# Writing down the order of GpSimd's work in the up-projection of a hybrid diffusion backbone

## The chip, the cores and the metric

The kernel runs on one core of a Trainium2 chip. The metric is device time in microseconds (us) of one execution. The engines are named as in the profile: PE (matrix products), DVE (VectorE), ACT (ScalarE), POOL (GpSimd) and SP, whose queue issues most DMAs. Each engine takes its own instructions in the order in which they stand in its stream, and waits at an instruction until the semaphores of that instruction are there.

## The reference, cut to what matters

One layer of a trunk over 2048 latent tokens of width 1024, with 256 tokens of context in front. All inputs are float32. The change lies in the last third of the layer, the gated MLP with a depthwise 3x3 convolution on the activation branch:

```python
def conv_ffn(h, w_up, taps, conv_b, w_down, rows):
    a, g = jnp.split(h @ w_up, 2, axis=-1)          # (2048, 1024) @ (1024, 2 * 2816)
    bsz, t, f = g.shape
    g2, tp = g.reshape(bsz, rows, GRID_W, f), taps  # rows of 64 tokens
    gc = lax.conv_general_dilated(g2, tp[:, :, None, :].astype(g.dtype), (1, 1), 'SAME',
                                  dimension_numbers=('NHWC', 'HWIO', 'NHWC'), feature_group_count=f)
    gc = gc.reshape(bsz, t, f) + conv_b
    return (a * jax.nn.gelu(gc, approximate=False)) @ w_down
```

## The kernel before

**Stages.** Input projection and the two token mixers (tiles `pj`, `sc`, `mi`), then the output projection with the second norm, then the up-projection `h @ w_up` (tiles `up`, `Ah`, `Al`), then the down-projection (tile `dn`, `mhl`, `thl`). Every product of two float32 matrices is made of three passes of a rounded type: each operand is split into a high part (a cast on ACT) and a low part (raw minus high), and high x high, high x low and low x high are summed in PSUM.

**The up-projection.** The tokens are done in two halves of 1024 (`hh` 0 and 1). Each half goes through 22 units, 11 of the gate `g` and 11 of the value `a`, each for 256 columns of `w_up`. A unit is a fast matrix product with seven products (`i` 0 to 6) in place of eight: column quarters of the weights, `a11`, `a12`, `a21`, `a22`, and sums of them are multiplied with stored combinations of the activations (`xah`, `xal`, `yfar`), 12 matmuls of 128x512 for each product. There are 308 products. A gate unit and a value unit run interleaved, 14 products for the two; such a stretch is called a **round** below. A round of 14 products makes the gate of two blocks of 128 channels and the value of the two blocks whose gate came out of the round two before.

**Preparing the weights** (`Unit.prep`, called three products ahead: `LOOK = 3`, four buffers each of `Ah` and `Al`). For product `i` of a unit ACT casts the operand to `Ah` (L125) and POOL subtracts it to get `Al` (L126). Besides, POOL makes the sums of quarters, in place: L1251 after `i` = 0, L1253 (`s2`, seen as tile `s` for a gate unit and `fl` for a value unit) after 1, L1255 (a11 = s2 + a11) after 2, L1257 (a12 = a12 - s2) after 3. The operand of `i` = 2 is `s2`; that of `i` = 3 is the a11 that L1255 leaves; that of `i` = 5 is the a12 that L1257 leaves.

**After a product** (`after`). DVE and ACT add the PSUM bank (four banks `up`) into the rows `gp` for the convolution (L1524) or into the value. Of a value unit, products `i` = 1 and 4 are multiplied with the gate on DVE (L1531, L1532); for `i` = 5 and 6 DVE adds (L1534) and POOL multiplies into the gate's tile `cv` (L1535), and the block is stored to `m`.

**The convolution** (`conv`). For each block of 128 channels ACT starts it with the first tap (L1433, into the PSUM tile `dn`, two buffers), DVE does the other eight taps (L1436), ACT applies the GELU (L1452 in the first half, L1457 in the second) into one of three tiles `cv`. In the second half DVE also makes three small edge taps (L1440) for each block. Each round has two of these convolutions.

**What sets the order.** The kernel's text emits all this in one sequence, but a scheduler places each engine's instructions by its own estimate, except those that are wrapped in `pin(...)` (`tc.keep_in_program_order`): these keep the order in which they are written among the pinned ones of their engine. Before the change on POOL in this stage L1253, the memset L1455 and the product of edges L1458 are pinned.

Of the kernel before, what the change touches and what calls it, by code (L numbers as in the profile page):

```python
# [9 lines left out]
F32 = mybir.dt.float32  # L10
# [67 lines left out]
def tile_trunk(ctx, tc, x, c, cx, c_ctx, w_ada, b_ada, norm_mix, norm_ffn, w_in, hg_norm, sgu_g, sgu_b,  # L78
               w_sp, b_sp, w_out, w_up, conv_w, conv_b, w_down, norm_final, masks, out):
    nc = tc.nc  # L80
    V, S, G, T = nc.vector, nc.scalar, nc.gpsimd, Tensor(nc.tensor)
    ld = nc.sync.dma_start
    st = nc.sync.dma_start
    pin = tc.keep_in_program_order
# [38 lines left out]
    def split(hi, lo, raw, eng=None, keep=lambda i: i):  # L123

        keep(S.copy(hi, raw))  # L125
        (eng or G).tensor_sub(lo, raw, hi.bitcast(F32))  # L126
# [57 lines left out]
    with es1:  # L184
# [169 lines left out]
        with tc.manual_schedule():  # L354
# [30 lines left out]
            for k in range(NK):  # L385
                for i in range(2):
                    o = (k % 2) * 256 + i * P
# [249 lines left out]
        def need(q, what):  # L637
            while what not in done:
                if hg_q.soon:
                    hg_q.flush()  # L640
                    continue
                assert q.tasks
                q.step()
# [531 lines left out]
        i = len(seq) - 4  # L1175
# [34 lines left out]
    def a_tiles():  # L1210
        return tuple(px.tile([P, 4, P], F32R, tag=w, name=w, bufs=4, align_bytes=AL) for w in ("Ah", "Al"))
# [4 lines left out]
    def c_tile():  # L1216
        return px.tile([P, NK, P], F32R, tag="fl", name="fl", bufs=2, align_bytes=AL)
# [5 lines left out]
    class Unit:  # L1223
# [15 lines left out]
        def prep(self, i):  # L1239

            a11, a21 = self.raw[0][:, :, :P], self.raw[0][:, :, P:]
            a12, a22 = (self.raw[1][:, :, :P], self.raw[1][:, :, P:]) if i else (None, None)
            self.A[i] = a_tiles()
            hi, lo = self.A[i]

            if i == 1:
                self.s2 = (c_tile()[:, :4, :].bitcast(F32) if self.slots[0] == 1 else
                           px.tile([P, 4, P], F32, tag="s1", name="s2"))
            split(hi, lo, (a11, a12, self.s2, a11, a21, a12, a22)[i])
            if i == 0:  # L1250
                G.tensor_sub(a21, a11, a21)  # L1251
            elif i == 1:
                pin(G.tensor_sub(self.s2, a22, a21))  # L1253
            elif i == 2:
                G.tensor_add(a11, self.s2, a11)  # L1255
            elif i == 3:
                G.tensor_sub(a12, a12, self.s2)  # L1257

    units = []
    for hh in range(2):  # L1260
# [25 lines left out]
    with tc.tile_pool(name="po", bufs=1, reuse_waits="tile") as po:  # L1286
# [62 lines left out]
        for t, (hh, g) in enumerate(tiles):  # L1349
# [15 lines left out]
            o = ops.pop(t)  # L1365
# [5 lines left out]
            if t + 1 == nt_:  # L1371
                for n in range(3):
                    prep(n)
# [36 lines left out]
    def g_rows(hh, f, n2):  # L1410

        return view(gp[f % 4], (1 + 2 * n2) * RW + 1, [[4 * RW, 4], [RW, 2], [1, GW]])

    def v_cols(hh, f, n2):
        return view(vals[hh, f], hh * GW + n2 * P, [[2 * P, 4], [1, P]])
# [4 lines left out]
    def edge(hh, f):  # L1420

        e = edges[:, f % 4]
        if hh:
            ld(e[:, 0, :], gs_d[f][:, 1, :])
            ld(e[:, 1, :], as_d[f])
        return e

    def conv(hh, f, e):

        gt = gp[f % 4]  # L1430
        cp = dbank().rearrange("p a b -> p (a b)")
        cr = cp.rearrange("p (r c) -> p r c", c=GW)
        S.activation(cr, gt[:, 0:RH, 0:GW], AF.Identity, bias=cvb[:, f:f + 1], scale=taps[:, f:f + 1])  # L1433
        yield
        for t in range(1, 9):
            V.scalar_tensor_tensor(out=cr, in0=gt[:, t // 3:t // 3 + RH, t % 3:t % 3 + GW],  # L1436
                                   scalar=taps[:, t * NF + f:t * NF + f + 1], in1=cr, op0=ALU.mult, op1=ALU.add)
            if hh and t == 4:
                for tt in range(6, 9):
                    V.scalar_tensor_tensor(out=e[:, 0, :], in0=gt[:, 1, tt % 3:tt % 3 + GW],  # L1440
                                           scalar=taps[:, tt * NF + f:tt * NF + f + 1], in1=e[:, 0, :],
                                           op0=ALU.mult, op1=ALU.add)
            if hh and t == 6:
                pin(S.activation(e[:, 0, :], e[:, 0, :], AF.Gelu))
            yield
        tapped.add((hh, f))
        while out_v[0] == 3:
            yield "full"
        out_v[0] += 1
        vt = v_tile()  # L1450
        if hh == 0:
            pin(S.activation(vt[:, :TH - GW], cp[:, :TH - GW], AF.Gelu))  # L1452
            S.copy(e[:, 0, :], cp[:, TH - GW:])
            S.dma_start(gs_d[f][:, 1, :], e[:, 0, :])
            pin(G.memset(vt[:, TH - GW:TH], 1.0))  # L1455
        else:
            pin(S.activation(vt[:, GW:], cp, AF.Gelu))  # L1457
            pin(G.tensor_mul(vt[:, :GW], e[:, 0, :], e[:, 1, :]))  # L1458
        vals[hh, f] = vt
        yield  # L1460
# [27 lines left out]
    def put_m(hh, f):  # L1488
        stores.append((now[0] + 3, hh, f))
# [13 lines left out]
    def quad(p, kind):  # L1503
        return p.rearrange("p (j c) -> p j c", c=P) if kind == "a" else p.rearrange("p (j r c) -> p j r c", r=2, c=GW)

    def after(u, i, p):

        hh, f, kind = u.hh, u.f, u.kind
        if i == 0:
            t = pf.tile([P, 2 * 512], F32, tag="keep", name="keep", bufs=2)  # L1510
            u.u, u.u3 = t[:, :512], t[:, 512:]
            S.copy(u.u, p)
            return
        if i == 2:
            V.tensor_add(u.u, p, u.u)
            return
        if i == 3:
            V.tensor_add(u.u3, p, u.u)
            return
        c, n2, add = {1: (0, 0, u.u), 4: (1, 1, u.u3), 5: (0, 1, u.u3), 6: (1, 0, u.u)}[i]  # L1520
        if kind == "g":
            if f >= 4:
                need(tapped, (hh, f + c - 4))
            V.tensor_add(g_rows(hh, f + c, n2), quad(p, kind), quad(add, kind))  # L1524
        else:
            need(vals, (hh, f + c))
            o = v_cols(hh, f + c, n2)
            if i < 5:
                if i == 4:
                    V.tensor_add(u.u, p, u.u)  # L1530
                V.tensor_add(p, p, add)  # L1531
                V.tensor_mul(o, quad(p, kind), o)  # L1532
            else:
                V.tensor_add(add, p, add)  # L1534
                G.tensor_mul(o, quad(add, kind), o)  # L1535
                put_m(hh, f + c)
        if kind == "g" and i == 4:
            V.tensor_add(u.u, p, u.u)
        if kind == "g" and i == 6:
            for ff in (f, f + 1):  # L1540
                if hh == 0:
                    st(gs_d[ff][:, 0, :], gp[ff % 4][:, RH, 1:GW + 1])
                else:
                    ld(gp[ff % 4][:, 0, 1:GW + 1], gs_d[ff][:, 0, :])
                fresh.append(conv(hh, ff, edge(hh, ff)))
# [41 lines left out]
    for n, (u, i) in enumerate(prods):  # L1587
# [5 lines left out]
        hi, lo = u.A[i]  # L1593
# [5 lines left out]
        if n == 12:  # L1599
            edges = px.tile([P, 7, P], F32R, tag="yst", name="edges", bufs=2, align_bytes=AL).bitcast(F32)  # L1600
            edges = edges[:, :4, :].rearrange("p f (w c) -> p f w c", w=2)
        after(u, i, p)
        put_stores(n)
        for j in range(7):
            if last_use[j] == n - 4:
                for w in range(2):
                    load_b(1, j, w)
        prep(n + LOOK)
        if n == NP - 8:
            ts = [c_tile().rearrange("p a b -> p (a b)").bitcast(F32) for i in range(2)]  # L1610
# [263 lines left out]
```

## Time and profile before

| what | us |
|---|---|
| median of 3 runs (2397.96 to 2403.45) | 2401.12 |
| the profiled execution: its own time | 2401.11 |
| its span, first to last instruction | 2399.3 |
| what lies around the span | 1.8 |
| first and last matmul of the up-projection, from the span's start | 1121.56, 1971.52 |
| granted clock of PE, mean | 0.994 |

All lines in the prediction are from this one profiled execution. A line of the timeline reads: start, length, engine, line of the kernel, operation, output and inputs, shape, and in brackets how long the engine stood idle just before and what it waited for. Two pieces of the same kind are often one line with a count (x2). A length contains a short tail that overlaps the next instruction, so the time that an instruction takes of its engine is better read from one start to the next.

### The profile page before, as it was taken

To read this page: it belongs to the slowest core of one execution; us is meant where nothing else is said; L and a number is where in the kernel's file an instruction comes from. 1 tells how busy PE (TensorE), PEld (TensorE's weight loads), DVE (VectorE), ACT (ScalarE), POOL (GpSimd) and SP (SyncE) were. 2 spreads that over 40 slices of the span, in tenths; PEclk is the share of its full clock that TensorE was granted. 3 is DMA by queue.
4 is the path that set the end of the run, shared out by engine and by line. 5 is a ranking of instruction groups with operands and counts; after the bars stand their busy time and mean duration, and the time that the engine had idled before them with its cause. 6 is when DMAs were issued, how large, how long until landed. Compare 5 with 4: busy or idle time off the path is not lost.

```text
span 2399.3 us, 38726 instructions
## 1 busy us (share of the span) xinstructions
PE 2347.8 (98%) x14951; PEld 1936.3 (81%) x14951; DVE 1705.8 (71%) x2331; ACT 977.3 (41%) x1762; POOL 798.4 (33%) x739
## 2 busy tenths in 40 slices
PE   6999999999999999999999999999999999999998
PEld 5887887878887887887788888887888888888887
DVE  4655667556668652666898787689999984776876
ACT  4674443443445452544433333333333333232343
POOL 0020000010211021004687877878787860000011
PEclk9999999999999999999999999999999999999999
DMA  8364443584435536678522222642222259844744
GB/s 307 120 199 151 141 124 126 167 279 153 159 128 178 188 110 222 202 242 289 185 85 92 82 92 93 242 172 85 87 95 87 86 175 343 269 145 134 251 154 168
DMA packets 305428, 396.39 MB, mean 165 GB/s; under 512 B 33609, under 2 KB 216657, under 8 KB 302557
## 3 DMA queue, kind: packets, MB, share of 16 engines
q1 hardware_dynamic: 301956, 393.17, 49.4%
q8 instruction: 118, 1.93, 0.3%
q10 hardware_dynamic: 3289, 0.76, 0.1%
q14 instruction: 65, 0.53, 0.1%
HBM read 284.73 MB, written 109.13 MB: 164 GB/s over the span
## 4 chain that ended last, share of the span: by engine, by line
PE 47%; DVE 4%; POOL 1%; issue 1%; DMA 0%; ACT 0%; POOLq 0%; SPq 0%; ACTq 0%
PE up L70 30%; PE dn L70 17%; DVE dn L1436 2%; POOL Al L126 0%; DVE edges L1440 0%; DVE gp L1524 0%; DMA m<-cv 0%; POOL cv L1535 0%; DMA sT<-wd 0%; POOL raw L1257 0%; DVE cv L1532 0%; DMA yd<-fl 0%; POOL fl L1253 0%; ACT cv L1457 0%; DVE up L1531 0%
## 5 line engine op out<-in xcount | busy, mean ns | idle before, releaser
L1436 DVE SCALAR_TENSOR_TENSOR dn<-gp,taps,dn 128x1024 f32<-128x1024 f32 x352 | 449.0, 1282 | 12.8 <-ACT dn L1433 9.6
L70 PE MATMUL up<-yfar,Ah 128*128 128x512 f32 x1232 | 394.3, 390 | 2.0 <-DVE cv L1532 2.0
L70 PE MATMUL dn<-thl,mhl 128*128 128x512 f32 x1680 | 381.0, 389 | 0.0
L70 PEld LDWEIGHTS dn<-thl,mhl 128*128 128x128 f32 x1680 | 315.4, 188 | 65.5 <-issue 0.2
L70 PE MATMUL pj<-xh,whi 128*128 128x512 f32 x896 | 367.7, 411 | 0.0
L126 POOL TENSOR_TENSOR Al<-raw,Ah 128x512 fp32r<-128x512 f32 x264 | 342.4, 1308 | 68.2 <-ACT Ah L125 67.9
L70 PE MATMUL pj<-xh,wlo 128*128 128x512 f32 x896 | 351.9, 393 | 2.1 <-DVE wlo L225 2.1
L70 PE MATMUL pj<-xl,whi 128*128 128x512 f32 x896 | 351.0, 392 | 0.0
L125 ACT CAST Ah<-raw 128x512 fp32r<-128x512 f32 x264 | 162.9, 620 | 334.9 <-PE up L70 261.3
L70 PE MATMUL up<-xah,Al 128*128 128x512 f32 x704 | 275.3, 391 | 3.6 <-POOL Al L126 3.6
L70 PE MATMUL up<-xah,Ah 128*128 128x512 f32 x704 | 275.2, 391 | 0.0
L70 PEld LDWEIGHTS up<-yfar,Ah 128*128 128x128 f32 x1232 | 231.5, 188 | 50.2 <-issue 2.4
L70 PE MATMUL up<-xal,Ah 128*128 128x512 f32 x528 | 205.8, 390 | 0.0
L70 PE MATMUL up<-yfar,Al 128*128 128x512 f32 x528 | 205.5, 390 | 0.0
L70 PEld LDWEIGHTS pj<-xh,wlo 128*128 128x128 f32 x896 | 168.6, 188 | 40.2 <-DVE wlo L225 3.6
L70 PEld LDWEIGHTS pj<-xh,whi 128*128 128x128 f32 x896 | 168.8, 188 | 35.1 <-issue 3.5
L70 PEld LDWEIGHTS pj<-xl,whi 128*128 128x128 f32 x896 | 169.1, 189 | 29.0
L70 PE MATMUL dn<-wo,o 128*128 128x512 f32 x768 | 182.7, 394 | 0.8 <-DVE nt L724 0.8
L70 PEld LDWEIGHTS dn<-wo,o 128*128 128x128 f32 x768 | 142.1, 188 | 30.0 <-DVE nt L724 1.0
L70 PEld LDWEIGHTS up<-xah,Al 128*128 128x128 f32 x704 | 132.6, 188 | 32.8 <-POOL Al L126 5.2
L70 PEld LDWEIGHTS up<-xah,Ah 128*128 128x128 f32 x704 | 132.6, 188 | 27.1
L222 ACT CAST whi<-raw 128x1024 fp32r<-128x1024 f32 x68 | 71.4, 1049 | 118.7 <-PE pj L70 96.7
(322 smaller groups left out, 3635.0 us busy)
## 6 DMA issues: line engine op xcount, KB each, us to landing
raw<-in_w_up_dram SPq DMA_DIRECT2D x88, 512.0 KB, 3.7
mr<-m SPq DMA_DIRECT2D x85, 512.0 KB, 5.3
raw<-in_w_in_dram SPq DMA_DIRECT2D x68, 512.0 KB, 4.0
sT<-wd SPq DMA_DIRECT2D x88, 256.0 KB, 4.4
raw<-in_w_ada_dram SPq DMA_DIRECT2D x32, 512.0 KB, 3.7
yfar<-yd SPq DMA_DIRECT2D x14, 1024.0 KB, 19.1
m<-cv SPq DMA_DIRECT2D x22, 544.0 KB, 2.7
raw<-in_w_down_dram SPq DMA_DIRECT2D x22, 512.0 KB, 4.2
```

Source lines behind the costliest of these rows:

```text
L70: return self.engine.matmul(out, lhsT, rhs, **kw)
L125: keep(S.copy(hi, raw))
L126: (eng or G).tensor_sub(lo, raw, hi.bitcast(F32))
L222: S.copy(hi, raw)
L1436: V.scalar_tensor_tensor(out=cr, in0=gt[:, t // 3:t // 3 + RH, t % 3:t % 3 + GW], scalar=taps[:, t * NF + f:t * NF + f + 1], in1=cr, op0=A ...
```

## The change

On POOL the low parts of the up-projection's weights, the three sums of quarters that were free, and the product of gate and value are now pinned, so that they follow the order in which the kernel writes them. No instruction is added or removed, and no operand changes. `split` is written out for this, since its subtraction had no pin.

```diff
-            split(hi, lo, (a11, a12, self.s2, a11, a21, a12, a22)[i])
+            S.copy(hi, (a11, a12, self.s2, a11, a21, a12, a22)[i])
+            pin(G.tensor_sub(lo, (a11, a12, self.s2, a11, a21, a12, a22)[i], hi.bitcast(F32)))
             if i == 0:
-                G.tensor_sub(a21, a11, a21)
+                pin(G.tensor_sub(a21, a11, a21))
             elif i == 1:
                 pin(G.tensor_sub(self.s2, a22, a21))
             elif i == 2:
-                G.tensor_add(a11, self.s2, a11)
+                pin(G.tensor_add(a11, self.s2, a11))
             elif i == 3:
-                G.tensor_sub(a12, a12, self.s2)
+                pin(G.tensor_sub(a12, a12, self.s2))
...
                 V.tensor_add(add, p, add)
-                G.tensor_mul(o, quad(add, kind), o)
+                pin(G.tensor_mul(o, quad(add, kind), o))
                 put_m(hh, f + c)
```

Lines behind L1249 have a number one higher in the changed kernel (L1251 becomes L1252, L1535 becomes L1536); the cast and the subtraction, L125 and L126 before, are L1249 and L1250 there.

The first place is POOL in the second half of the up-projection, around the two products of gate and value at the end of a round (`cv<-keep,cv`). `Al_17006` is the low part for `i` = 2 of the next gate unit, `raw_16844` the first quarters of the value unit that is being prepared, `fl_17032` its `s2`. Before:

```order
L126 TENSOR_TENSOR Al_16984<-raw_16844,Ah_16983 128x512
L1535 TENSOR_TENSOR cv_16526<-keep_16732,cv_16526 128x4x128
L126 TENSOR_TENSOR Al_17006<-s2_16961,Ah_17005 128x512
L126 TENSOR_TENSOR Al_17031<-raw_16942,Ah_17030 128x512
L1253 TENSOR_TENSOR fl_17032<-raw_16942,raw_16844 128x512
L1255 TENSOR_TENSOR raw_16844<-fl_17032,raw_16844 128x4x128
L1257 TENSOR_TENSOR raw_16942<-raw_16942,fl_17032 128x4x128
L1535 TENSOR_TENSOR cv_16800<-keep_16732,cv_16800 128x4x128
```

And in the changed kernel, the same place:

```order
L1536 TENSOR_TENSOR cv_16526<-keep_16732,cv_16526 128x4x128
L1250 TENSOR_TENSOR Al_16960<-raw_16868,Ah_16959 128x512
L1254 TENSOR_TENSOR s2_16961<-raw_16868,raw_16779 128x512
L1250 TENSOR_TENSOR Al_16984<-raw_16844,Ah_16983 128x512
L1252 TENSOR_TENSOR raw_16844<-raw_16844 128x4x128
L1536 TENSOR_TENSOR cv_16800<-keep_16732,cv_16800 128x4x128
L1250 TENSOR_TENSOR Al_17006<-s2_16961,Ah_17005 128x512
L1256 TENSOR_TENSOR raw_16779<-s2_16961,raw_16779 128x4x128
L1250 TENSOR_TENSOR Al_17031<-raw_16942,Ah_17030 128x512
L1254 TENSOR_TENSOR fl_17032<-raw_16942,raw_16844 128x512
L1250 TENSOR_TENSOR Al_17055<-raw_16779,Ah_17054 128x512
L1258 TENSOR_TENSOR raw_16868<-raw_16868,s2_16961 128x4x128
```

Behind these rows stand `Al_17076` (from `fl_17032`) and then the sum L1256 on `raw_16844`. So the first product (`cv_16526`) moved ahead of two low parts that it stood behind, the second (`cv_16800`) ahead of `Al_17006` and `Al_17031`, which stood in front of it, and the value unit's sum on `raw_16844`, two instructions ahead of the second product before, now stands eight instructions behind it and thirteen behind the first. The first half has the same rows in the same order.

The second place is ACT just behind, in the changed kernel; `Ah_17115` is the cast of `raw_16844` as L1256 leaves it, and `dn_17123` the next convolution:

```order
L1249 CAST Ah_17095<-raw_16779 128x512
L1249 CAST Ah_17115<-raw_16844 128x512
L1458 ACTIVATE cv_17120<-dn_16803 128x1024
L1434 ACTIVATE dn_17123<-gp1_11526,vec_67,taps_68 128x1024
L1249 CAST Ah_17139<-raw_16868 128x512
```

Nothing moved here: in the kernel before the five rows stand in the same order. On ACT in all, the cast of `s2` and a neighbour change places four times. DVE's order is the same from its first instruction to its last, and PE's differs in the place of one matmul.

The third place is POOL near the start of the up-projection, in the second round. Before:

```order
L126 TENSOR_TENSOR Al_11930<-raw_11815,Ah_11929 128x512
L1253 TENSOR_TENSOR fl_11931<-raw_11815,raw_11721 128x512
L1255 TENSOR_TENSOR raw_11721<-fl_11931,raw_11721 128x4x128
L1257 TENSOR_TENSOR raw_11815<-raw_11815,fl_11931 128x4x128
L126 TENSOR_TENSOR Al_11954<-raw_11685,Ah_11953 128x512
```

And in the changed kernel:

```order
L1250 TENSOR_TENSOR Al_11930<-raw_11815,Ah_11929 128x512
L1254 TENSOR_TENSOR fl_11931<-raw_11815,raw_11721 128x512
L1250 TENSOR_TENSOR Al_11954<-raw_11685,Ah_11953 128x512
L1258 TENSOR_TENSOR raw_11795<-raw_11795,s2_11855 128x4x128
L1250 TENSOR_TENSOR Al_11975<-fl_11931,Ah_11974 128x512
```

The low part `Al_11954` stood behind all three sums of the value unit, and now stands behind the first of them.

## The prediction

> **What bounds the kernel now.** I read the page first, its shares and its 40 slices:
>
> ```profile
> PE 2347.8 (98%) x14951; PEld 1936.3 (81%) x14951; DVE 1705.8 (71%) x2331; ACT 977.3 (41%) x1762; POOL 798.4 (33%) x739
> ...
> DVE  4655667556668652666898787689999984776876
> ...
> POOL 0020000010211021004687877878787860000011
> ```
>
> PE is the bound of the whole span. POOL's 33% is an average that hides the stage: in slices 20 to 33 (60 us each), which are the up-projection, POOL is 60 to 80% busy and DVE up to 90% and more. The change touches only that stage. Two stretches of one round's length, one in each half:
>
> ```profile
> 1332.00:1370.00 38.00, 38.00 (x169) 31.50 (x168) 29.89 (x32) 13.95 (x22) 30.49 (x27) 1.00 0.27 86
> ...
> 1794.00:1832.00 38.00, 38.00 (x169) 31.48 (x168) 34.90 (x39) 14.20 (x22) 30.82 (x27) 1.00 0.28 90
> ```
>
> After the length come the busy times of PE, PEld, DVE, ACT and POOL. PE has no gap; POOL has 7.5 us of 38 to spare, DVE 8.1 and then 3.1. So there is next to nothing to win in the middle of the stage. What PE loses to POOL is in the groups and in PE's own waits:
>
> ```profile
> L70 PE MATMUL up<-yfar,Ah 128*128 128x512 f32 x1232 | 394.3, 390 | 2.0 <-DVE cv L1532 2.0
> ...
> L70 PE MATMUL up<-xah,Al 128*128 128x512 f32 x704 | 275.3, 391 | 3.6 <-POOL Al L126 3.6
> ...
> 1179.90 0.50 PE L70 MATMUL up<-xah,Al 128*128 128x512 f32 x1 [1.77 <-POOL Al L126]
> ...
> 1564.50 0.50 PE L70 MATMUL up<-xah,Al 128*128 128x512 f32 x1 [1.62 <-POOL Al L126]
> ```
>
> POOL is waited for 3.6 us in all, DVE 2.0. That 5.6 us, 0.23%, is the most that a better order can win here.
>
> **The change part by part.** No instruction comes or goes, so busy times stay; every term is a wait. I name the steps of a round: E1 and E2 are DVE's adds L1534 after the value unit's products `i` = 5 and 6; M1 and M2 POOL's products L1535 that need them; R the value unit's sum L1255, whose result ACT casts; C the convolution's start L1433, which stands behind that cast on ACT; S the first tap L1436 on DVE, which needs C.
>
> *Removed.* The waits at 1179.90 and 1564.50 come from a low part that stands behind three sums in a row; in the new order the sums stand between the low parts, so both fall away: -3.4 us.
>
> *Added: a loop.* The order rows show that M1, which must wait for E1, now stands thirteen instructions ahead of R, and M2 eight ahead. Before, R stood ahead of M2 and only four behind M1. R releases the cast, the cast stands ahead of C, C releases S, and DVE works in order from S to the next round's E1 and E2. That is a closed ring through DVE, POOL and ACT, once a round. It costs nothing while it is shorter than PE's round. First half:
>
> ```profile
> 1298.98 2.61 DVE L1436 SCALAR_TENSOR_TENSOR dn<-gp,taps,dn 128x1024 f32<-128x1024 f32 x2
> ...
> 1309.26 0.69 DVE L1524 TENSOR_TENSOR gp<-up,keep 128x512 f32<-128x512 f32 x1 [0.38 <-PE up L70]
> ...
> 1317.22 0.39 PE L70 MATMUL up<-xah,Ah 128*128 128x512 f32 x1
> ...
> 1317.42 0.69 DVE L1534 TENSOR_TENSOR keep<-up,keep 128x512 f32<-128x512 f32 x1
> ...
> 1321.61 1.31 POOL L1535 TENSOR_TENSOR cv<-keep,cv 128x512 f32<-128x512 f32 x1
> 1322.87 1.31 POOL L126 TENSOR_TENSOR Al<-s,Ah 128x512 fp32r<-128x512 f32 x1
> ...
> 1333.56 0.62 ACT L125 CAST Ah<-raw 128x512 fp32r<-128x512 f32 x1 [1.86 <-PE up L70]
> ...
> 1335.56 1.21 ACT L1433 ACTIVATE dn<-gp,vec,taps 128x1024 f32<-128x1024 f32 x1 [0.41 <-ACT edges L1453]
> ...
> 1337.06 2.61 DVE L1436 SCALAR_TENSOR_TENSOR dn<-gp,taps,dn 128x1024 f32<-128x1024 f32 x2
> ...
> 1714.12 0.68 DVE L1534 TENSOR_TENSOR keep<-up,keep 128x512 f32<-128x512 f32 x1
> ...
> 1714.88 1.30 POOL L1535 TENSOR_TENSOR cv<-keep,cv 128x512 f32<-128x512 f32 x1 [0.57 <-DVE keep L1534]
> ```
>
> PE's round is the time between the two first taps, 1298.98 and 1337.06: 38.08 us, or 2.72 for a product. DVE from S (1298.98) to the end of E1 (1318.11) takes 19.13, less 0.38 and 0.20 in which it waited for PE (the product ended at 1317.22): 18.55. POOL from M1 to the end of R is 14 instructions of 1.26 (the starts 1321.61 and 1322.87): 17.6. ACT from the cast to the end of C (1336.77): 3.21. Handing over costs 0.08 to POOL (1714.80 to 1714.88), and 0.03 to DVE (1835.84 to 1835.87 in the rows further down), which I take for ACT too. Sum 39.5: **longer than PE's round by 1.4 us**. PE itself feels it when M1's delay uses up the slack of the low part seven instructions on (`i` = 2 of the gate unit): it is done 0.69 + 0.08 + 7 x 1.26 = 9.6 us after E1's start. It is due for the third matmul, 0.45 us into the product that starts 4 x 2.72 after 1317.22; E1 started 0.20 after that, so it is due after 10.88 + 0.45 - 0.20 = 11.1 us: slack 1.5.
>
> ```profile
> 1242.97 0.69 DVE L1534 TENSOR_TENSOR keep<-up,keep 128x512 f32<-128x512 f32 x1
> ...
> 1507.82 0.69 DVE L1534 TENSOR_TENSOR keep<-up,keep 128x512 f32<-128x512 f32 x1
> ```
>
> These are E1 of the second and of the ninth round that have one: seven rings, 264.9 us now and 7 x 39.5 = 276.5 in the changed kernel, +11.6; less the slack of 1.5, and less 2 us because the second round's E1 comes earlier without the wait at 1179.90 (its 1.77 and a little idle time): **+8 us**, with that wait's end in it.
>
> In the second half M2 closes the longer ring, since three edge taps lie between E1 and E2:
>
> ```profile
> 1797.79 1.29 DVE L1436 SCALAR_TENSOR_TENSOR dn<-gp,taps,dn 128x1024 f32<-128x1024 f32 x1 [1.16 <-ACT dn L1433]
> ...
> 1808.74 0.69 DVE L1524 TENSOR_TENSOR gp<-up,keep 128x512 f32<-128x512 f32 x1 [0.58 <-PE up L70]
> ...
> 1815.55 1.28 DVE L1436 SCALAR_TENSOR_TENSOR dn<-gp,taps,dn 128x1024 f32<-128x1024 f32 x1
> ...
> 1816.90 0.69 DVE L1534 TENSOR_TENSOR keep<-up,keep 128x512 f32<-128x512 f32 x1
> ...
> 1822.14 0.39 PE L70 MATMUL up<-xah,Ah 128*128 128x512 f32 x1
> ...
> 1826.09 0.68 DVE L1534 TENSOR_TENSOR keep<-up,keep 128x512 f32<-128x512 f32 x1
> ...
> 1833.05 0.62 ACT L125 CAST Ah<-raw 128x512 fp32r<-128x512 f32 x1 [1.89 <-PE up L70]
> ...
> 1834.63 1.21 ACT L1433 ACTIVATE dn<-gp,vec,taps 128x1024 f32<-128x1024 f32 x1
> ...
> 1835.87 1.29 DVE L1436 SCALAR_TENSOR_TENSOR dn<-gp,taps,dn 128x1024 f32<-128x1024 f32 x1 [1.16 <-ACT dn L1433]
> ```
>
> DVE already waits for C here in the kernel before (1.16 us), so there is no cover left. S to the end of E2 (1826.77) is 28.98, less 0.58 and some 0.15 of waiting for PE ahead of E1 (it starts 1.35 after a tap, where the taps of 1298.98 have 1.2 to 1.3 each): 28.2. POOL from M2 to the end of R, 9 instructions: 11.3. ACT from cast to the end of C (1835.84): 2.8. Handing over 0.14. Sum 42.5, 4.4 above the round. The edge taps can give some of it back:
>
> ```profile
> L1440 DVE SCALAR_TENSOR_TENSOR edges<-gp,taps,edges x66: 272/1212/1400, 1563.3 to 1937.8; 128x64 f32<-128x64 f32 x66
> ...
> 1644.99 0.28 DVE L1440 SCALAR_TENSOR_TENSOR edges<-gp,taps,edges 128x64 f32<-128x64 f32 x1
> ```
>
> One takes 0.27 to 1.40 us for the same shape. In the new order POOL ends M1 and the four instructions behind it 0.68 + 0.08 + 5 x 1.26 = 7.1 us after E1's start and then stands idle for M2, and the third of the three edge taps falls there: I take 0.9 us off (1.21 less 0.28), 41.6, and as ends 42.5 (none) and 39.5 (all three at 0.28). The Trainium skill, "SBUF — State Buffer", section "SBUF: two separate sides", has DVE operations with two SBUF inputs and GpSimd operations exclude each other for a whole instruction; the spread of L1440, which has two, agrees, and by that rule the 0.9 is right, while without it the ring stays at 42.5.
>
> The ring does not bind at the start of the second half, where DVE is behind on its own and taps start well after C:
>
> ```profile
> 1682.29 1.21 ACT L1433 ACTIVATE dn<-gp,vec,taps 128x1024 f32<-128x1024 f32 x1
> ...
> 1685.91 1.28 DVE L1436 SCALAR_TENSOR_TENSOR dn<-gp,taps,dn 128x1024 f32<-128x1024 f32 x1
> ...
> 1940.34 0.68 DVE L1534 TENSOR_TENSOR keep<-up,keep 128x512 f32<-128x512 f32 x1
> ```
>
> C of the third round ends at 1683.50, its taps begin 2.4 us later. So I count from E2 of the third round (1714.12, above) to that of the ninth (1940.34): 226.2 now; then six rings of 41.6, less 0.8 for the shorter DVE stretch of the first: 248.8, +22.6. Besides, E2 now starts (1826.09) 3.95 after its product's end (1822.14), and two products after that end, so 5.44 - 3.95 = 1.5 after E2's start, PE begins the product whose low part will stand behind M2. Then it can begin only 0.68 + 0.08 + 2 x 1.26 - 0.45 = 2.8 after E2's start: +1.3. The last convolutions start late by the same ring, and the stage ends a little later still: 0 to 8 us, I take 3. Second half **+27 us**.
>
> *Moved besides.* Four pairs on ACT and, around the change of halves, some loads on SP's queue by one or two places: a preparation has three products, 8 us, in hand, so nothing. If that cover is gone, one late load costs PE at most what it costs POOL now, some 2 us.
>
> **Sum:** +8 +27 -1.6 (the wait at 1564.50) = +33 on a span of 2399.3, with 1.8 around it: 2434 us. The profiled execution, 2401.11, is the median of the runs to 0.01, so nothing is corrected.
>
> I read POOL's time from start to start. The Trainium skill, "Perfetto Trace Analysis", section "GPSIMD Engine Instruction", calls a GpSimd span unreliable and says to use that spacing. With the reported 1.31 of the two rows the rings would be 40.2 and 42.1, and the time about 2441.
>
> **Rivals.**
> 1. *The rings are cut by something that I have not seen*, say DVE finds the next taps ready. Then only the direct wait through M2 is left, +1.3 us once or a few times, against the 3.4 that fall away: about 2400, no change. For it: the sum of the first half is only 1.4 above the round, within the reading of three engines. Against: in the second half it is 3.5 above, and DVE's wait for C stands in the row at 1797.79.
> 2. *Faster.* The interleaved sums free PE from all waits for POOL, and, with the products of gate and value done early, from the one for DVE's L1532: -5.6 us, 2395.5. It decides at a ring of 38.08: below that M1 and M2 wait in POOL's spare time of 7.5 us. It would need 1.4 us less in one half and 3.5 in the other; the DVE stretches alone are 18.6 and 28.2 us of operations that no order shortens.
> 3. *Slower still:* the rings stand at 39.5 and 42.5, the early rounds of the second half, where E2 is later, bind too, and the end costs 8: +10 (nothing off at the start) +39 -1.6 = 2448.
>
> That nothing moves is excluded by the order rows.
>
> **How the numbers follow.** My forecast with its spread has 0.72, the third case 0.12, the first 0.10, the second 0.06. Forecast 2434. The spread: with a ring of 39.5 in the second half too and nothing at the end, 6 x 39.5 - 0.8 - 226.2 = +10 there, +8 +10 +1.3 -1.6, 2419; with 42.5 and 8 at the end, +8 +28 +1.3 +8 -1.6, 2445. I widen downwards a little towards the first case: 2408 to 2450. About 0.2% (4.8 us) is what a measurement of this kernel tells from no change: faster 0.05, same 0.09, slower 0.86.
>
> **What would show it.** Right: PE's waits for POOL's `Al` rise from 3.6 to some 30 us, most of them one a round, about 1.5 us in the first half and 3 to 4 in the second; POOL waits for L1534 in nearly every round; DVE waits for C (L1433) every round, and first taps lie 39.5 and 41 to 42 us apart. The 1.77 and 1.62 are gone. Wrong: first taps still 38.1 apart, or DVE idle for anything but C, or the time lost at the change of halves or outside the stage.

## The result

| | us |
|---|---|
| before, median of 4 runs (2397.96 to 2403.45) | 2401.86 |
| changed, median of 4 runs (2442.95 to 2446.03) | 2444.03 |
| ratio changed to before, 95% interval | 1.0179, 1.0161 to 1.0197 |
| forecast, and its range | 2434, 2408 to 2450 |
| span of the profiled execution, before and changed | 2399.3, 2444.2 |

The change costs 42 us; the forecast was 33.

### The profile after

The page of the changed kernel: the engines, DVE and POOL in 40 slices (of 61 us here), and the group that stood at 3.6 us of waiting for POOL before:

```profile
PE 2364.1 (97%) x14951; PEld 1936.6 (79%) x14951; DVE 1712.3 (70%) x2331; ACT 970.0 (40%) x1762; POOL 797.4 (33%) x739
...
DVE  4656677556767743656986868599989884676876
...
POOL 0020000000201120005778787867676760000011
...
L70 PE MATMUL up<-xah,Al 128*128 128x512 f32 x704 | 281.2, 400 | 25.4 <-POOL Al L1250 25.3
```

POOL's busy time is what it was (798.4 before), and in slices 26 to 32 (counted from 0), the second half of the up-projection, POOL is at 60 to 70% where it was at 70 to 80%: less loaded, in a longer time. PE waits for POOL's `Al` 25.3 us in this group instead of 3.6. The view of all waits (total us, times, longest) has the two waits that feed that one:

```profile
POOL cv L1536 <- DVE keep L1535: 121.2, 29, 8.1
...
DVE dn L1437 <- ACT dn L1434: 59.1, 18, 4.8
...
PE up L70 <- POOL Al L1250: 28.6, 33, 2.5
```

They were 5.3, 9.6 and 3.6 us before. That is a circle by names: POOL waits for DVE's add, DVE for ACT's start of a convolution, and ACT, in the rows below, for POOL's sum. Busy times over one round of either half, between two E1 of the first half and two E2 of the second:

```profile
1322.60:1361.96 39.36, 38.69 (x170) 31.39 (x169) 29.70 (x33) 13.47 (x22) 30.44 (x26) 1.00 0.26 84
1856.32:1897.68 41.36, 38.89 (x165) 31.69 (x164) 35.43 (x40) 13.89 (x22) 30.78 (x26) 0.96 0.26 83
...
1860.20:1863.60 3.40, 3.40 (x10) 2.63 (x9) 3.11 (x3) 0.89 (x2) 3.40 (x4) 0.50 0.11 43
```

A round lasts 39.36 and 41.36 us instead of 38.08, and no engine is busy through it: POOL has 8.9 and 10.6 us idle, DVE 9.7 and 5.9. PE's 38 us of work wait with them.

The third stretch lies just behind PE's longest wait in the second (2.47 us, the row at 1859.62 below). The granted clock is 0.50 there, and the matmuls start 0.43 us apart instead of 0.23, which costs PE some 1.4 us. The changed kernel has five such stretches in this stage, from 1686 on, that the kernel before does not have; they are part of why PE is busy 16 us longer (2347.8 before) with the same matmuls. They do not set the round: from E2 to E2 it lasts 41.36 to 41.40 us in the three rounds with one (from 1773.51, 1856.32 and 1939.10) and 41.39 to 41.43 in the three without. The last, 4 us ahead of the end of the stage, has nothing behind it that could take it up. The timeline shows one ring of the first half link by link, then the marks of the second half:

```profile
1243.86 0.69 DVE L1535 TENSOR_TENSOR keep<-up,keep 128x512 f32<-128x512 f32 x1
...
1322.60 0.69 DVE L1535 TENSOR_TENSOR keep<-up,keep 128x512 f32<-128x512 f32 x1
...
1323.37 1.30 POOL L1536 TENSOR_TENSOR cv<-keep,cv 128x512 f32<-128x512 f32 x1 [4.85 <-DVE keep L1535]
...
1339.64 1.30 POOL L1256 TENSOR_TENSOR raw<-fl,raw 128x512 f32<-128x512 f32 x1
...
1340.97 0.62 ACT L1249 CAST Ah<-raw 128x512 fp32r<-128x512 f32 x1 [3.38 <-POOL raw L1256]
...
1342.96 1.21 ACT L1434 ACTIVATE dn<-gp,vec,taps 128x1024 f32<-128x1024 f32 x1 [0.40 <-ACT edges L1454]
...
1344.21 2.62 DVE L1437 SCALAR_TENSOR_TENSOR dn<-gp,taps,dn 128x1024 f32<-128x1024 f32 x2 [3.27 <-ACT dn L1434]
...
1361.96 0.69 DVE L1535 TENSOR_TENSOR keep<-up,keep 128x512 f32<-128x512 f32 x1
...
1519.66 0.69 DVE L1535 TENSOR_TENSOR keep<-up,keep 128x512 f32<-128x512 f32 x1
...
1683.15 0.69 DVE L1535 TENSOR_TENSOR keep<-up,keep 128x512 f32<-128x512 f32 x1
...
1732.12 0.68 DVE L1535 TENSOR_TENSOR keep<-up,keep 128x512 f32<-128x512 f32 x1
...
1856.32 0.68 DVE L1535 TENSOR_TENSOR keep<-up,keep 128x512 f32<-128x512 f32 x1
...
1859.62 0.50 PE L70 MATMUL up<-xah,Al 128*128 128x512 f32 x1 [2.47 <-POOL Al L1250]
...
1980.50 0.68 DVE L1535 TENSOR_TENSOR keep<-up,keep 128x512 f32<-128x512 f32 x1
```

E1 starts at 1322.60; M1, idle until then for 4.85 us, 0.77 later; R thirteen places on, 16.27 later, 1.25 a place; the cast, which had waited 3.38 us for R, at 1340.97; C 1.99 later, behind a GELU that stands between the two; S 1.25 after C, when DVE had waited 3.27 us for it; the next E1 17.75 after S. The sum is 39.36, and no link has slack. E1 of the second round to E1 of the ninth, 1243.86 to 1519.66, is 275.80 us (264.85 before), seven rings of 39.40. E2 of the third to E2 of the ninth round of the second half, 1732.12 to 1980.50, is 248.38 (226.22 before), six rings of 41.40.

### The profile page after: what moved, and what is told of

Read it like the earlier page. It is cut to its first block, busy times and chain, and to the rows that moved or that the text cites. A ratio compares the mean times of both kernels' runs of the same rounds, so it can differ in the third digit from the quotient of the medians.

```text
span 2444.2 us, 38651 instructions
## 1 busy us (share of the span) xinstructions
PE 2364.1 (97%) x14951; PEld 1936.6 (79%) x14951; DVE 1712.3 (70%) x2331; ACT 970.0 (40%) x1762; POOL 797.4 (33%) x739
## 4 chain that ended last, share of the span: by engine, by line
PE 39%; issue 6%; POOL 6%; DVE 1%; DMA 0%; ACT 0%; POOLq 0%; SPq 0%; ACTq 0%; DVEq 0%
PE up L70 22%; PE dn L70 17%; POOL Al L1250 4%; POOL s L1254 1%; DVE dn L1437 1%; POOL raw L1252 1%; POOL cv L1536 0%; DMA m<-cv 0%; ACT Ah L1249 0%; POOL raw L1258 0%; DVE gp L1525 0%; DMA raw<-m 0%; DVE fl L126 0%; POOL fl L1254 0%; DMA as<-cv 0%
## 5 line engine op out<-in xcount | busy, mean ns | idle before, releaser
L1250 POOL TENSOR_TENSOR Al<-raw,Ah 128x512 fp32r<-128x512 f32 x264 | 342.8, 1308 | 97.9 <-ACT Ah L1249 83.1
L70 PE MATMUL up<-xah,Al 128*128 128x512 f32 x704 | 281.2, 400 | 25.4 <-POOL Al L1250 25.3
L1249 ACT CAST Ah<-raw 128x512 fp32r<-128x512 f32 x264 | 160.0, 618 | 316.8 <-POOL raw L1256 169.0
L70 PEld LDWEIGHTS up<-yfar,Al 128*128 128x128 f32 x528 | 99.5, 188 | 25.8 <-POOL Al L1250 5.1
```

Of the source, the lines that this page charges most:

```text
L70: return self.engine.matmul(out, lhsT, rhs, **kw)
L1249: S.copy(hi, (a11, a12, self.s2, a11, a21, a12, a22)[i])
L1250: pin(G.tensor_sub(lo, (a11, a12, self.s2, a11, a21, a12, a22)[i], hi.bitcast(F32)))
```

## Experiments

R's distance on POOL is given in places behind M1 and M2: 4 and ahead of M2 in the kernel before, 13 and 8 in the changed one. The pin on the product of gate and value changes nothing by itself: with that pin alone all five engines have the order of the kernel before, and with all pins but that one the order of the changed kernel.

| run | R behind M1, M2 | us | ratio to before, 95% interval |
|---|---|---|---|
| changed kernel | 13, 8 | 2444.03 | 1.0179, 1.0161 to 1.0197 |
| e1: low parts alone pinned | 11, 5 | 2416.26 | 1.0064, 1.0052 to 1.0077 |
| e2: sums alone pinned | 9, 4 | 2395.99 | 0.9986, 0.9978 to 0.9995 |
| e3: R written earlier | 10, 4 | 2410.01 | 1.0044, 1.0031 to 1.0056 |
| e4: cast behind C on ACT | 13, 8 | 2411.82 | 1.0045, 1.0032 to 1.0059 |
| e5: products written later | 7, 4 | 2401.72 | 1.0005, 0.9996 to 1.0014 |
| e6: e5 with R earlier | 3, ahead of M2 | 2399.60 | 0.9995, 0.9986 to 1.0004 |
| e7: R one place earlier | 12, 7 | 2427.99 | 1.0108, 1.0094 to 1.0122 |
| e8: one more operation ahead of R | 14, 9 | 2466.94 | 1.0275, 1.0259 to 1.0292 |

How far PE is behind the kernel before, in us, at the first matmul of a product (12 matmuls each), both counted from the first matmul of the stage, is worked out from the traces:

| product (its start in the kernel before) | changed | e1 | e2 | e3 | e4 | e5 | e6 | e7 | e8 |
|---|---|---|---|---|---|---|---|---|---|
| 28 (1205.70) | -1.3 | -2.1 | -2.9 | -1.8 | -3.2 | -3.1 | -2.2 | -3.1 | -3.0 |
| 140 (1510.34) | 7.0 | 0.5 | -2.9 | 1.2 | -2.5 | -3.1 | -2.2 | -1.4 | 16.3 |
| 196 (1666.96) | 9.8 | 1.2 | -5.7 | 2.1 | -2.3 | 0.5 | -4.7 | 0.3 | 22.8 |
| 210 (1705.15) | 14.8 | 6.4 | -5.7 | 6.9 | 2.7 | 2.1 | -4.8 | 4.6 | 26.0 |
| 224 (1743.26) | 19.6 | 7.5 | -5.7 | 6.9 | 9.0 | 2.0 | -4.9 | 10.0 | 32.3 |
| 294 (1933.66) | 37.6 | 10.8 | -5.7 | 7.1 | 9.0 | 2.0 | -4.9 | 20.5 | 55.7 |
| last matmul (1971.52) | 44.0 | 12.6 | -5.7 | 9.3 | 12.1 | 3.2 | -3.8 | 24.8 | 65.3 |

The profiled execution of e5 took 2409.39 us, 7.7 above its median; 5.9 us of that lie ahead of the stage, which begins at 1127.46.

### e1 and e2: one kind of pin alone

e1, against the changed kernel:

```diff
-                pin(G.tensor_sub(a21, a11, a21))
+                G.tensor_sub(a21, a11, a21)
...
-                pin(G.tensor_add(a11, self.s2, a11))
+                G.tensor_add(a11, self.s2, a11)
...
-                pin(G.tensor_sub(a12, a12, self.s2))
+                G.tensor_sub(a12, a12, self.s2)
...
-                pin(G.tensor_mul(o, quad(add, kind), o))
+                G.tensor_mul(o, quad(add, kind), o)
```

> Only the low parts (Al) are pinned; the three sums and the product of gate and value are left free as before. POOL's order then has R eleven behind M1 and five behind M2 (in the changed kernel thirteen and eight), and the low part for i = 2 of the gate unit still directly behind M2. Theory of the closed ring: the changed kernel's rings measure 39.36 us (first half) and 41.4 (second) at 1.25 a place, so here 39.36 - 2 x 1.25 = 36.9 and 41.4 - 3 x 1.25 = 37.65, both under PE's 38.08: no price, 2396 to 2402 us, ratio to before 0.998 to 1.001. Rival 'direct wait' (PE stands at the low part behind M2, whatever the ring): nearly all of the loss stays, 2430 or more. Rival 'each pin costs its share': some 2415 to 2430.

e2:

```diff
-            S.copy(hi, (a11, a12, self.s2, a11, a21, a12, a22)[i])
-            pin(G.tensor_sub(lo, (a11, a12, self.s2, a11, a21, a12, a22)[i], hi.bitcast(F32)))
+            split(hi, lo, (a11, a12, self.s2, a11, a21, a12, a22)[i])
...
-                pin(G.tensor_mul(o, quad(add, kind), o))
+                G.tensor_mul(o, quad(add, kind), o)
```

> Only the three sums are pinned; the low parts and the product are left free. R stands nine behind M1 and four behind M2. Theory of the closed ring: 39.36 - 4 x 1.25 = 34.4 and 41.4 - 4 x 1.25 = 36.4, open: 2396 to 2402 us. Rival 'each pin costs its share': what the low parts don't cost, so that the two kernels' losses add up to about 42 us.

Two parts that cost 16 and -4 us against the kernel before cost 42 together, so no pin has a share of its own. e2 went as the ring says, and is faster than both kernels: its groups have no wait of PE for POOL left in this stage.

```profile
L70 PE MATMUL up<-xah,Al 128*128 128x512 f32 x704 | 274.0, 389 | 0.1
...
L70 PE MATMUL up<-yfar,Al 128*128 128x512 f32 x528 | 205.3, 389 | 0.0
```

e1 missed: 2416 where the ring gave 2396 to 2402. Its timeline in the second half has another, shorter ring:

```profile
1832.51 0.68 DVE L1535 TENSOR_TENSOR keep<-up,keep 128x512 f32<-128x512 f32 x1
...
1834.53 1.28 POOL L1250 TENSOR_TENSOR Al<-s,Ah 128x512 fp32r<-128x512 f32 x1
...
1835.86 0.50 PE L70 MATMUL up<-xah,Al 128*128 128x512 f32 x1 [0.34 <-POOL Al L1250]
...
1841.07 0.62 ACT L1249 CAST Ah<-raw 128x512 fp32r<-128x512 f32 x1 [1.11 <-PE up L70]
1842.65 1.21 ACT L1434 ACTIVATE dn<-gp,vec,taps 128x1024 f32<-128x1024 f32 x1
...
1843.89 1.29 DVE L1437 SCALAR_TENSOR_TENSOR dn<-gp,taps,dn 128x1024 f32<-128x1024 f32 x1 [1.18 <-ACT dn L1434]
...
1871.26 0.68 DVE L1535 TENSOR_TENSOR keep<-up,keep 128x512 f32<-128x512 f32 x1
```

R no longer holds the cast; PE does, whose product had waited for the low part directly behind M2. E2 to E2 is 38.75, 0.67 over PE's round: some 3.3 us from product 224 to 294 in the table. This ring is read from the rows; no run cuts it. The rest, 5 us of it between products 196 and 210, is no ring: it comes once.

### e3 and e4: the ring cut at two other places

e3 leaves all pins and both products where the change put them, and writes R earlier:

```diff
             elif i == 1:
                 pin(G.tensor_sub(self.s2, a22, a21))
-            elif i == 2:
                 pin(G.tensor_add(a11, self.s2, a11))
```

> Everything pinned as in the changed kernel, but the sum a11 = s2 + a11 is written right behind s2, one preparation earlier. R stands ten behind M1 and four behind M2; both products stay where the change put them. Theory of the closed ring: 39.36 - 3 x 1.25 = 35.6 and 41.4 - 4 x 1.25 = 36.4, open: 2394 to 2401 us, first taps 38.1 apart in both halves, PE's waits for POOL's Al under 5 us. Rivals 'direct wait behind M2' and 'POOL in a fixed order waits for DVE': 2430 or more, since POOL still waits at M1 and M2 in written order.

e4 leaves POOL's distances alone and takes the cast that needs R from ahead of C:

```diff
-        prep(n + LOOK)
+        for m in (n + LOOK - 1, n + LOOK):
+            if m < len(prods) and ((prods[m][0].kind, prods[m][1]) == ("a", 3)) == (m < n + LOOK):
+                prep(m)
```

> The changed kernel with the preparation of the value unit's i = 3 one product later, so that on ACT the cast that needs R stands behind C instead of ahead of it; POOL keeps M1, M2 and R in the changed kernel's distances. Theory of the closed ring: cut at ACT, C then hangs only on the cast of s2, four places ahead of R on POOL, 39.36 - 5.0 = 34.4 and 41.4 - 5.0 = 36.4, open: 2396 to 2405 us (in one round at the start of the second half the cast still stands ahead of C, up to 6 us). Rivals with the cause on POOL alone (direct wait, fixed order): 2440 or more, since POOL's order around M1, M2 and R is the changed kernel's.

Both take away some 31 of the 42 us, one by a move on POOL, one by a move on ACT; a price on POOL alone would have stayed in e4. (The edit of e4 also moves some taps and adds on DVE by a place or two, so it is not a cut at ACT alone; e7 and e8 below leave DVE's and ACT's order as it is.) In the steady rounds next to nothing is left (table: 28 to 140 in e4, 224 to 294 in both). But they missed their ranges, by 9 and 7 us, and the table says where: between products 196 and 210, about 5 us in e1, e3, e4 and the changed kernel alike; at the change of halves; at the end; and in e4 between 210 and 224, 6.3 us. The last is not the round that the expectation of e4 had left out: there the cast of R, at 1643.20, stands ahead of C, at 1645.75, and DVE does not wait for it. It follows a late E1, whose cause stands under "The step that failed". The timeline of e3 behind E1 of the second round of the second half (1671.59):

```profile
1672.35 1.28 POOL L1535 TENSOR_TENSOR cv<-keep,cv 128x512 f32<-128x512 f32 x1 [8.11 <-DVE keep L1534]
...
1674.91 0.50 PE L70 MATMUL up<-xah,Al 128*128 128x512 f32 x1 [1.99 <-POOL Al L1250]
...
1678.76 0.50 PE L70 MATMUL up<-xah,Al 128*128 128x512 f32 x1 [1.29 <-POOL Al L1250]
...
1682.50 0.50 PE L70 MATMUL up<-xah,Al 128*128 128x512 f32 x1 [0.68 <-POOL Al L1250]
```

DVE is late there with its first convolutions and edge taps. M1 stands 8.11 us at the head of POOL's queue, and the low parts that PE needs stand behind it. So a second theory: what the ring leaves is POOL held at M1 or M2 while DVE is late. Its rival: the low parts' own pins, since e2, without them, is the only run so far that has no rest.

### e5 and e6: the products written later

```diff
-                pin(G.tensor_mul(o, quad(add, kind), o))
-                put_m(hh, f + c)
+                late.append((now[0] + (2 if i == 5 else 1), now[0] + 3, o, quad(add, kind), hh, f + c))
...
         prep(n + LOOK)
+        put_late(n)
```

`put_late(n)` writes those that are due, each with its pin, and enters its store at the place that it had. DVE's order stays that of the changed kernel; ACT's is that of the kernel before.

> Everything pinned as in the changed kernel, but the products of gate and value are written later: M1 behind the preparation two products on, M2 behind that one product on; the stores keep their place. R then stands seven behind M1 and four behind M2, and the low parts that the next products need stand ahead of M1 and M2. The kernels with low parts alone pinned, with the sum earlier and with the cast behind C were all left 10 to 16 us over the kernel before, and PE's waits for POOL that are left lie at the start of a half, at its first convolutions and at its end, where DVE is behind and POOL stands at M1 for up to 8.1 us. Theory 'the rest is POOL held at M1 or M2 while DVE is late': gone here, 2393 to 2400 us, PE's waits for POOL's Al in all under 4 us. Rival 'the rest is the pins of the low parts themselves' (the kernel without them was the only one without the rest): stays, 2408 to 2415.

e6 adds e3's edit (R stands three places behind M1 there, not the four that its expectation counted).

> The products written later, as in the run beside it, and the sum a11 = s2 + a11 written right behind s2: R stands four behind M1 and ahead of M2's next rows, so that no ring can be closed at all. Theory: as the run beside it or up to 2 us less, 2392 to 2399 us. Rival 'pins of the low parts': 2408 to 2415.

With all pins in place the rest is gone: from e3 to e6, which differ by where the products are written, the ratio falls from 1.0044 to 0.9995, some 12 us. PE's waits for `Al` are 1.7 us in e5 and 3.9 in e6, 12.7 in e3. That decides against the pins of the low parts as its cause. In its profiled execution e5 still loses 3.6 us between products 140 and 196, where an edge tap on DVE stands for 10.60 us; e6 has no such tap (more on these below). Both came 0.6 to 1.7 us above their ranges and can't be told from the kernel before. Whether the pins of the low parts cost the 2 to 4 us by which e2 is better stays open, since the intervals of e2 and e6 overlap.

### e7 and e8: one place less, one place more

e7 writes R ahead of the low part for `i` = 2, in value units:

```diff
+            if i == 2 and self.kind == "a":
+                pin(G.tensor_add(a11, self.s2, a11))
             pin(G.tensor_sub(lo, (a11, a12, self.s2, a11, a21, a12, a22)[i], hi.bitcast(F32)))
+            if i == 2 and self.kind == "g":
+                pin(G.tensor_add(a11, self.s2, a11))
```

> The changed kernel with the value unit's sum R written one place earlier on POOL, ahead of the low part of i = 2: R stands twelve behind M1 and seven behind M2. Theory of the closed ring: one place is 1.25 us of the ring, so 39.36 - 1.25 = 38.11 in the first half (0.03 over PE's round instead of 1.28, seven rounds: 8.7 us less) and 41.4 - 1.25 = 40.15 in the second (seven rounds: 8.7 less): 2444 - 17.5 = 2426.5 us, 2422 to 2431. Rival 'direct wait behind M1 and M2 at a fixed price': M1 and M2 stand where they did, 2441 to 2447.

e8:

```diff
             elif i == 2:
+                if self.kind == "a":
+                    pin(G.tensor_sub(lo, self.s2, hi.bitcast(F32)))
                 pin(G.tensor_add(a11, self.s2, a11))
```

> The changed kernel with one more POOL operation a round: the low part of the value unit's i = 2 is computed twice, so that R stands fourteen behind M1 and nine behind M2. Theory of the closed ring: rings of 40.6 and 42.65, 1.25 us more in each of seven rounds of either half: 2444 + 17.5 = 2461.5 us, 2457 to 2467, although POOL has 7 us to spare in a round. Rival 'direct wait at a fixed price', POOL's spare time takes it: 2443 to 2447.

2428.0 against 2426.5 expected, and 2466.9 against 2461.5. E1 and E2 in the timeline of e7, at the same rounds as above:

```profile
1239.16 0.69 DVE L1537 TENSOR_TENSOR keep<-up,keep 128x512 f32<-128x512 f32 x1
...
1506.19 0.69 DVE L1537 TENSOR_TENSOR keep<-up,keep 128x512 f32<-128x512 f32 x1
...
1718.67 0.68 DVE L1537 TENSOR_TENSOR keep<-up,keep 128x512 f32<-128x512 f32 x1
...
1959.79 0.68 DVE L1537 TENSOR_TENSOR keep<-up,keep 128x512 f32<-128x512 f32 x1
```

And in that of e8:

```profile
1242.64 0.69 DVE L1537 TENSOR_TENSOR keep<-up,keep 128x512 f32<-128x512 f32 x1
...
1527.77 0.69 DVE L1537 TENSOR_TENSOR keep<-up,keep 128x512 f32<-128x512 f32 x1
...
1741.56 0.68 DVE L1537 TENSOR_TENSOR keep<-up,keep 128x512 f32<-128x512 f32 x1
...
1998.02 0.68 DVE L1537 TENSOR_TENSOR keep<-up,keep 128x512 f32<-128x512 f32 x1
```

Seven rings of the first half last 38.15 us each in e7, 39.40 in the changed kernel, 40.73 in e8; six of the second 40.19, 41.40 and 42.74. That is 1.2 to 1.35 us a place in both halves, for an engine with 9 us idle in each round. At 38.15 the loss of the first half is almost gone: the point from which it counts is PE's 38.08, as the second rival had it.

## Why the prediction was right, and where it was short

By its own steps, with the starts of the rows above and of the prediction. The stage begins 2.2 us later in this profiled execution of the changed kernel (its first matmul at 1123.77, 1121.56 before), which is ahead of all that the change touches and is taken off in the first line.

| step | forecast | measured |
|---|---|---|
| first half, to E1 of the ninth round | +8 | 1519.66 - 1507.82 - 2.2 = +9.64 |
| change of halves, to E2 of the second round | -1.6 | (1683.15 - 1671.49) - (1519.66 - 1507.82) = -0.18 |
| E2 of the second to the third round | 0 | (1732.12 - 1683.15) - (1714.12 - 1671.49) = +6.34 |
| E2 of the third to the ninth round | +22.6 | 248.38 - 226.22 = +22.16 |
| PE behind M2, and the end | +1.3 +3 | 44.9 of the span less 1980.50 - 1940.34 = +4.74 |
| sum | +33 | +42.70 |

The row of the kernel before that the third step needs, E2 of the second round, is this one of its timeline, with E1 of that round ahead of it:

```profile
1669.71 0.68 DVE L1534 TENSOR_TENSOR keep<-up,keep 128x512 f32<-128x512 f32 x1
...
1671.49 0.68 DVE L1534 TENSOR_TENSOR keep<-up,keep 128x512 f32<-128x512 f32 x1
```

**What bounds.** Right: PE's 38.08 a round is the line that a ring has to cross. "The most that a better order can win here", 5.6 us, is right in size too: e2 wins 3.9.

**The rings.** The mechanism was right and its size too: 39.5 and 41.6 forecast, 39.4 and 41.4 measured; e4, e7 and e8 show it as a cause.

**The waits that go.** The 1.77 and 1.62 are gone, as said; e2 shows what they are worth when nothing replaces them, 2.9 us by product 28 and 5.7 by product 196, more than the 3.4 of the two rows. In the changed kernel POOL stands still for a product of gate and value at the change of halves too, and PE gets small waits in place of the second:

```profile
1551.96 1.30 POOL L1536 TENSOR_TENSOR cv<-keep,cv 128x512 f32<-128x512 f32 x1 [6.10 <-DVE keep L1535]
...
1561.54 0.50 PE L70 MATMUL up<-yfar,Al 128*128 128x512 f32 x1 [0.68 <-POOL Al L1250]
...
1576.42 10.82 DVE L1441 SCALAR_TENSOR_TENSOR edges<-gp,taps,edges 128x64 f32<-128x64 f32 x3
...
1587.94 0.70 PE L70 MATMUL up<-yfar,Ah 128*128 128x512 f32 x2 [1.48 <-ACT Ah L1249]
```

The largest, 1.48 us, comes from DVE, as far as the rows show. ACT, which the row names, had ended its last cast at 1586.97, but DVE's add of a PSUM bank at 1587.15 ended 0.1 us ahead of PE's start; it had stood behind three edge taps, of which the first alone lasted 10.18 us. So the -1.6 became -0.2.

**The step that failed** is "The ring does not bind at the start of the second half, where DVE is behind on its own", with the 2.4 us between C's end and its taps as the reason. It put the step from the second to the third E2 at nothing, and that step cost 6.3 us. The slack was read in the old order and for M2 alone. E1 of that round is as late as E2 (1669.71 and 1671.49), and M1, which needs E1, stands thirteen places ahead of R. With the prediction's own terms C would end at 1669.71 + 0.69 + 0.08 + 17.6 + 3.2 = 1691.3, more than 5 us behind the first taps at 1685.91; the sum could have been made. In the changed kernel DVE does wait for that C, 2.43 us. But the late C does not settle how long the step lasts. An edge tap stands right behind it. In the changed kernel:

```profile
1702.50 1.29 DVE L1437 SCALAR_TENSOR_TENSOR dn<-gp,taps,dn 128x1024 f32<-128x1024 f32 x1 [2.43 <-ACT dn L1434]
1703.70 4.12 DVE L1441 SCALAR_TENSOR_TENSOR edges<-gp,taps,edges 128x64 f32<-128x64 f32 x1
```

The same tap in e4, then in e7:

```profile
1685.82 7.05 DVE L1441 SCALAR_TENSOR_TENSOR edges<-gp,taps,edges 128x64 f32<-128x64 f32 x1
```

```profile
1689.03 5.34 DVE L1443 SCALAR_TENSOR_TENSOR edges<-gp,taps,edges 128x64 f32<-128x64 f32 x1
```

From the second to the third E2 it is 48.97 us in the changed kernel, 48.95 in e7, whose R is a place earlier, and 48.96 in e4, where DVE does not wait for this C at all. What the three share is the end of that tap, 26.4 us after E1 of the second round: it stands while POOL, held at M1 for 8.1 us, works off without a gap what had queued up behind. In e1, e3 and e6, where no edge tap is longer than 1.41 us, the step takes 45.10, 43.39 and 42.51 (42.63 before). In e8 C comes so late (DVE waits 4.20 us) that its tap takes 1.33, and the step 48.39. So a late E1, which holds M1, delays the next one in two ways, by the ring and by the edge tap, and the later of the two counts; the prediction had neither here. The next E1 is late by it, and PE's waits between products 210 and 224 in the changed kernel, e4 and e7 follow from that. Besides, PE felt M1 directly, as e3 shows where the ring is open: there the 5 us between products 196 and 210 are all still there. Rival 3, 2448, had these rounds bind, by longer rings than were measured; it came nearest in time, not by this mechanism.

**The 0.9 for the edge taps.** Right in size, wrong in place, so it was luck that the 41.6 came out so near. In the changed kernel:

```profile
1890.18 1.28 POOL L1536 TENSOR_TENSOR cv<-keep,cv 128x512 f32<-128x512 f32 x1 [4.85 <-DVE keep L1535]
...
1891.21 0.34 DVE L1441 SCALAR_TENSOR_TENSOR edges<-gp,taps,edges 128x64 f32<-128x64 f32 x1
...
1892.67 1.38 DVE L1441 SCALAR_TENSOR_TENSOR edges<-gp,taps,edges 128x64 f32<-128x64 f32 x1
1892.68 1.28 POOL L1254 TENSOR_TENSOR s<-raw 128x512 f32<-128x512 f32 x1
```

It is the first of the three taps that is short, because it begins just ahead of the end of M1. The third is still 1.40: POOL is not idle by then.

**The signs.** PE's waits for `Al`, 28.6 us for "some 30", and the distances of the taps were right. "Most of them one a round" was half right: in the first half it is two, of 0.2 and 0.5 us, where a ring costs 1.3; in the second one of 2.5 and one of 1.4 in turn, not 3 to 4, with PE at the clock of 0.50 behind the longer. One sign of being wrong came true in part: 6.3 of the 42.7 us were lost near the change of halves.

**Faster** had 0.05, and was far off for this change. That its idea holds where no ring closes is shown by e2.

## What to carry to other kernels

An instruction that waits for another engine is not free because its own engine has time to spare: count, for each such instruction in a fixed order, which later instruction of its queue another engine waits for, follow the chain back to the start, and compare its length with the period of the bound engine; beyond that, each place costs its full length every round. Pinning all of an engine's work in the written order does this silently, and two pins that cost little apart can close a ring together. Read the slack of such a ring anew in the rounds where an engine is late, since a late producer holds the whole queue behind its consumer, and the work that the queue then does without a gap can hold up another engine (an edge tap of 10.18 us here).

## What the runs showed of the hardware

An edge tap of 64 elements takes 0.27 us at best, and its length depends on where in a POOL instruction it starts: 0.34 us when started 1.03 us into one of 1.28, 1.38 when started together with one (1892.67 and 1892.68). In both cases it ends within 0.1 us of POOL's instruction. It can be much longer. The line of these taps in the changed kernel, with the shortest, the median and the longest in ns:

```profile
L1441 DVE SCALAR_TENSOR_TENSOR edges<-gp,taps,edges x66: 271/1204/10180, 1576.4 to 1978.0; 128x64 f32<-128x64 f32 x66
```

The longest, from 1576.42 to 1586.60, stood through eight POOL instructions without a gap between them (1576.46 to 1586.51) and ended 0.1 us behind the last. Taps of 4.0 to 10.6 us stand in the changed kernel, e4, e5, e7 and e8, each ending 0.1 us behind the end of a POOL instruction; in the kernel before, e1, e2, e3 and e6 none is longer than 1.41. What lets some taps in behind one instruction of such a row, like the one at 1892.67, and others not, no run shows. The convolution's taps, whose output and one input are in PSUM, keep to 1.28 beside POOL. The Trainium skill, "SBUF — State Buffer", section "SBUF: two separate sides", has a DVE operation with two SBUF inputs and a GpSimd operation exclude each other for the whole instruction; the short taps agree, and the long ones were shut out for several. No run was made to take POOL away from a tap.
